# One core, x·W − sub: another order of the transfers, and an eighth pair of tiles transposed on VectorE

## Chip, cores and metric

One NeuronCore of a Trainium2 chip runs the whole kernel. The metric is the device time of one execution in microseconds; the figure shown is the median of several runs.

## What is computed

```
batch, m, k, n = 16, 512, 1024, 768
x (batch, m, k), weight (k, n), sub_value (batch, m, n), all float32
out = (np.matmul(x, weight) - sub_value).astype(np.float32)
```

x, read as 8192 rows of 1024, is 33.6 MB; weight is 3.1 MB; sub_value and out are 25.2 MB each. Together 87.03 MB cross between HBM and SBUF.

## The kernel before

**Tiles.** The 8192 rows are 64 tiles of 128 rows, numbered 0 to 63. Eight tiles (a group of 1024 rows) are interleaved, so that partition p holds eight neighbouring rows of a group, and a transfer of n tiles of one group moves n·4 KB (x) or n·3 KB (sub_value, out) per partition in one packet.

**Work of a tile.** A tile of x lands as float32 in `x_ring` (16 slots). ScalarE casts it to f16 (`cast`, L295). Then it has to be transposed, in one of two ways. On TensorE: four matmuls against an identity (`transposes`, L313; two f16 move as one float32 word) into PSUM `pt_b`, and ScalarE copies the result to `xt_b` (L320, "evac"). Or on VectorE: the tiles whose pair begins in `ON_DVE` are transposed two at a time by sixteen 32-row stream transposes (`transposes_dve`, L340) from `x16p_b` to `xtp_b`. Then TensorE does 16 matmuls of 128x384 (`matmuls`, L364 weight loads and L176 matmuls) with the f16 weight in `w_sb`, into one of three PSUM buffers `po_b` (NPO = 3). VectorE subtracts (`finish`, L384) in place in `so_ring` (32 slots of 128x768), where sub_value had landed, and the slot is then written out.

**Order on TensorE.** The first three tiles follow the weight chunks by hand, with idle matmuls (L401, L414) that fill waits. From tile 3 on, the four transposes of tile mi + 2 stand between the four quarters of the matmuls of tile mi. A tile of a VectorE pair has no transposes on TensorE. Casts are queued 4 tiles ahead of their use, those of a VectorE pair 7 tiles ahead (`lead`). The sixteen stream transposes of a pair are put on VectorE's queue four at a time (PER = 4), each four behind a `finish`, starting at tile (pair − 6).

**Order of the transfers.** One list, `TRANSFERS`, names every DMA in order: kind (x, w, s for sub_value, o for out), first tile, number of tiles. SyncE issues them all, in this order, on one queue (L240 for w, L276 for the others). An x transfer waits until the casts of the tiles that had its slots are done; an s transfer waits until the o transfer that had its slots has landed; an o transfer waits for the `finish` of its tiles. Whatever stands behind a waiting transfer in the list waits too. The first four weight chunks are staged in the last slots of `so_ring`.

**End.** Transfers share semaphores (`lane`). SyncE waits at the end for all output transfers but the last, then the program's closing steps run, and the last transfer is waited for behind them.

Of the kernel before, what the change touches and what calls it, by code (L numbers as in the profile page):

```python
# [19 lines left out]
LEAD_DVE = 7  # L20
PER = 4
HEAD = 3
ON_DVE = frozenset(range(18, 60, 6))
LOOP = None

TRANSFERS = [
    ('x', 0, 1), ('w', 0, 1), ('x', 1, 1), ('w', 1, 1), ('x', 2, 1), ('w', 2, 1),
    ('w', 3, 1), ('x', 3, 2), ('s', 0, 1), ('x', 5, 3), ('s', 1, 3), ('x', 8, 3),
    ('s', 4, 4), ('x', 11, 5), ('s', 8, 8), ('x', 16, 8), ('x', 24, 3), ('s', 16, 8),
    ('x', 27, 5), ('o', 0, 8), ('s', 24, 8), ('x', 32, 8), ('s', 32, 8), ('o', 8, 8),  # L30
    ('x', 40, 8), ('s', 40, 8), ('x', 48, 8), ('o', 16, 8), ('o', 24, 8), ('s', 48, 8),
    ('x', 56, 8), ('s', 56, 8), ('o', 32, 8), ('o', 40, 8), ('o', 48, 8), ('o', 56, 4),
    ('o', 60, 2), ('o', 62, 1), ('o', 63, 1),
]


# [66 lines left out]
def kernel(  # L103
# [174 lines left out]
    def cast(mi):  # L278
# [4 lines left out]
        waits = [landed["x", mi]]  # L283
        if first in ON_DVE:
            if mi == first:
# [14 lines left out]
    def transposes(mi):  # L300
        def one(c):
            def f():
                waits = []
                if c == 0:
                    b, before = take("pt", NPT, mi)
                    waits.append((counter["cast"], cast_at[mi]))
                    if before is not None:
                        waits.append((counter["evac"], evac_at[before]))
                b = slot["pt", mi]
                words = pt_b[:, b].bitcast(F32)[:, c * P : (c + 1) * P]  # L310
                from_ = x16_b[:, slot["x16", mi]].bitcast(F32)[:, c * P : (c + 1) * P]
                last = c == n_c - 1
                pe.add(lambda: nc.tensor.transpose(words, from_, ident), waits, count("turn") if last else None)  # L313
                if last:
                    turn_at[mi] = so_far["turn"]
                    d, before = take("xt", NXT, mi)
                    waits = [(counter["turn"], turn_at[mi])]
                    if before is not None:
                        waits.append((counter["mul"], mul_at[before]))
                    act.add(lambda: nc.scalar.copy(out=xt_b[:, d], in_=pt_b[:, b]), waits, count("evac"))  # L320
                    evac_at[mi] = so_far["evac"]
            return f
        return [one(c) for c in range(n_c)]

    def transposes_dve(mi):

        x16 = x16p_b[:, slot["x16p", mi]].bitcast(F32).rearrange("p j (c q) -> p (j c) q", c=n_c)
        blocks = [(a, b) for a in range(P // Q) for b in range(P // Q)]

        def one(n, a, b):  # L330
            def f():
                waits = []
                if n == 0:
                    d, before = take("xtp", NXTP, mi)
                    waits.append((counter["cast"], cast_at[mi + 1]))
                    if before is not None:
                        waits.append((counter["mul"], mul_at[before + 1]))
                xt = xtp_b[:, slot["xtp", mi]].bitcast(F32).rearrange("p j (c m) -> p (j c) m", c=n_c)
                last = n == len(blocks) - 1
                dve.add(lambda: nc.vector.transpose(  # L340
                    xt[b * Q : (b + 1) * Q, :, a * Q : (a + 1) * Q],
                    x16[a * Q : (a + 1) * Q, :, b * Q : (b + 1) * Q],
                ), waits, count("pair") if last else None)
                if last:
                    pair_at[mi] = so_far["pair"]
            return f
        return [one(n, a, b) for n, (a, b) in enumerate(blocks)]

    def matmuls(mi, c):
        first = mi - mi % 2  # L350
        on_dve = first in ON_DVE
        waits = []
# [26 lines left out]
    def finish(mi):  # L379
        assert mi in done["s"]  # L380
        done["finish"].add(mi)
        o = so_ring[:, mi % NSO].rearrange("p (h n) -> p h n", h=2)
        po = po_b[:, slot["po", mi]]
        dve.add(lambda: nc.vector.tensor_tensor(  # L384
            out=o, in0=po[:, :, :NS], in1=o, op=mybir.AluOpType.subtract
        ), [landed["s", mi], (counter["mul"], mul_at[mi])], count("finish"))
        finish_at[mi] = so_far["finish"]
        issue()
# [16 lines left out]
    def lead(mi):  # L405
        return LEAD_DVE if mi - mi % 2 in ON_DVE else TA + CA

# [38 lines left out]
    for mi in range(HEAD, n_mt):  # L446
# [3 lines left out]
        t = mi + TA  # L450
        tr = transposes(t) if t < n_mt and t - t % 2 not in ON_DVE else []
        for c in range(n_c):
# [6 lines left out]
        finish(mi)  # L459
        if mi + LEAD_DVE - 1 in ON_DVE:  # L460
            waiting += transposes_dve(mi + LEAD_DVE - 1)
# [55 lines left out]
```

## Time and profile before

| what | us |
|---|---|
| median of 3 runs (210.75, 210.76, 211.0) | 210.76 |
| the profiled execution's own time | 211.0 |
| span of that execution in the trace | 208.9 |
| TensorE busy (share of the span) | 197.5 (95%) |
| VectorE busy | 114.0 (55%) |
| ScalarE busy | 113.0 (54%) |
| the data queue (q1), share of the 16 DMA engines' span | 97.9% |
| mean rate of all transfers | 417 GB/s |

The span runs from the first to the last instruction in the trace; 2.1 us of the execution's time lie outside it. Busy times of TensorE are longer than the pace at which matmuls follow each other, because matmuls overlap: a 128x384 matmul shows 326 ns, and 36 of them end to end take 5.85 us in the chain of work, which is 0.163 us each. "Landing" of a transfer is the time at which the last of its 16 parts (one for each DMA engine) has told of its end.

### The profile page before, as it was taken

The page shows a single profiled execution, that of the slowest core. Times are in us where ns is not written, and L with a number is a line of the kernel's source. Part 1 is how long each engine was busy: PE and PEld are TensorE (multiplying, and loading weights), DVE is VectorE, ACT ScalarE, POOL GpSimd, SP SyncE. Part 2 cuts the span into 40 slices and gives each one's busy share as a digit, 9 for nine tenths or more (in the row PEclk, how much of TensorE's full clock was granted, in tenths as well). Part 3 has the DMA queues.
Part 4 walks back from the last instruction along what each step waited for, and adds up shares of the span by engine and source line. Part 5 has one row for each costly group of instructions (what it writes and reads, how often), then busy time and mean ns, then how long its engine had stood idle before and what let it go on. Part 6 is the DMA issues. An engine that isn't in the chain of part 4 may idle for free.

```text
span 208.9 us, 2462 instructions
## 1 busy us (share of the span) xinstructions
PE 197.5 (95%) x1250; PEld 80.1 (38%) x738; DVE 114.0 (55%) x186; ACT 113.0 (54%) x115; POOL 0.7 (0%) x6
## 2 busy tenths in 40 slices
PE   7898799999979999999999999999999999999991
PEld 2432244444333344344344334434434433444430
DVE  0342225106149849929956965992994796332331
ACT  3645665575396274655727628465572751755510
POOL 1000000000000000000000000000000000000000
PEclk9999999999999999999999999999999999999999
DMA  6999999999999999999999999999999999999994
GB/s 209 422 425 425 423 436 431 438 439 436 394 449 421 440 417 425 445 445 406 422 438 438 434 425 442 439 409 438 423 427 445 439 422 431 419 425 442 423 386 192
DMA packets 5626, 87.17 MB, mean 417 GB/s; under 512 B 624, under 2 KB 624, under 8 KB 2032
## 3 DMA queue, kind: packets, MB, share of 16 engines
q1 hardware_dynamic: 5616, 87.03, 97.9%
q8 instruction: 7, 0.11, 0.2%
q14 instruction: 3, 0.02, 0.0%
HBM read 61.87 MB, written 25.17 MB: 417 GB/s over the span
## 4 chain that ended last, share of the span: by engine, by line
PE 68%; DMA 18%; DVE 5%; SPq 3%; ACT 1%; issue 1%; DVEq 0%; ACTq 0%
PE po_b L176 61%; DMA so_ring<-in_sub_value_dram 18%; PE pt_b L313 7%; DVE xtp_b L340 3%; SPq L276 2%; DVE so_ring L384 2%; SPq L240 1%; ACT xt_b L320 0%; ACT x16p_b L295 0%; ACT x_b L295 0%; SPq L512 0%; DVEq L56 0%; ACTq L56 0%; SPq L130 0%
## 5 line engine op out<-in xcount | busy, mean ns | idle before, releaser
L176 PE MATMUL po_b<-w_sb,xt_b 128*128 128x384 f16 x800 | 145.7, 326 | 1.9 <-ACT xt_b L320 1.4
L384 DVE TENSOR_TENSOR so_ring<-po_b,so_ring 128x768 f32<-128x768 f32 x64 | 60.7, 956 | 60.7 <-PE po_b L176 40.1
L320 ACT COPY xt_b<-pt_b 128x1024 f16<-128x1024 f16 x50 | 50.6, 1012 | 72.7 <-PE pt_b L313 72.1
L364 PEld LDWEIGHTS <-xt_b 128*128 128x128 f16 x400 | 39.2, 98 | 58.9 <-issue 53.6
L340 DVE STREAM_TRANSPOSE xtp_b<-x16p_b 32x256 f32<-32x256 f32 x112 | 48.8, 436 | 19.1 <-ACT x16p_b L295 17.3
L313 PE MATMUL pt_b<-ident,x_b 128*128 128x128 f32 x200 | 52.4, 274 | 3.1 <-ACT x_b L295 2.9
L295 ACT CAST x_b<-x_ring 128x1024 f16<-128x1024 f32 x50 | 51.6, 1048 | 6.5 <-DMA x_ring<-in_x_dram 6.5
L313 PEld LDWEIGHTS pt_b<-ident,x_b 128*128 128x128 f32 x200 | 27.5, 141 | 46.8 <-issue 40.4
L176 PE MATMUL po_b<-w_sb,xtp_b 128*128 128x384 f16 x224 | 42.9, 326 | 0.3 <-DVE xtp_b L340 0.3
L295 ACT CAST x16p_b<-x_ring 128x1024 f16<-128x1024 f32 x14 | 14.6, 1046 | 7.0 <-DMA x_ring<-in_x_dram 7.0
L364 PEld LDWEIGHTS <-xtp_b 128*128 128x128 f16 x112 | 11.0, 98 | 13.2 <-issue 11.2
L243 DVE CAST w_sb<-so_ring 128x768 f16<-128x768 f32 x8 | 4.1, 556 | 10.4 <-DMA so_ring<-in_weight_dram 10.4
L401 PE MATMUL po_b<-idle_x,idle_w 128*128 128x512 f16 x25 | 7.5, 449 | 1.5 <-DVE idle_x L395 1.5
L401 PEld LDWEIGHTS po_b<-idle_x,idle_w 128*128 128x128 f16 x25 | 2.7, 112 | 4.6 <-issue 1.9
L295 ACT ACT_TABLE_LOAD x1 | 1.3, 1283 | 0.9 <-SPq L130 0.9
L394 DVE MEMSET idle_w<- 128x64 uint32 x1 | 0.1, 112 | 1.0 <-SPq L130 1.0
L414 PE MATMUL po_b<-idle_x,idle_w 128*128 128x512 f16 x1 | 0.4, 379 | 0.0
L165 POOL TENSOR_SCALAR_AFFINE_SELECT ident<-ident 128x128 f32<-128x128 f32 x1 | 0.3, 294 | 0.1
L395 DVE MEMSET idle_x<- 128x256 uint32 x1 | 0.3, 272 | 0.0
L164 POOL MEMSET ident<- 128x128 f32 x1 | 0.2, 206 | 0.5 <-SPq L130 0.5
L414 PEld LDWEIGHTS po_b<-idle_x,idle_w 128*128 128x128 f16 x1 | 0.1, 98 | 0.1
L501 POOL MEMSET const-bfloat16-1.0<- 128x1 bf16 x1 | 0.1, 102 | 0.0
(3 smaller groups left out, 0.3 us busy)
## 6 DMA issues: line engine op xcount, KB each, us to landing
so_ring<-in_sub_value_dram SPq DMA_DIRECT2D x7, 3072.0 KB, 24.5
out_dram<-so_ring SPq DMA_DIRECT2D x7, 3072.0 KB, 31.2
x_ring<-in_x_dram SPq DMA_DIRECT2D x5, 4096.0 KB, 22.8
x_ring<-in_x_dram SPq DMA_DIRECT2D x2, 2560.0 KB, 26.2
x_ring<-in_x_dram SPq DMA_DIRECT2D x3, 1536.0 KB, 22.4
so_ring<-in_weight_dram SPq DMA_DIRECT2D x4, 768.0 KB, 8.5
x_ring<-in_x_dram SPq DMA_DIRECT2D x3, 512.0 KB, 6.1
so_ring<-in_sub_value_dram SPq DMA_DIRECT2D x1, 1536.0 KB, 26.3
```

Source lines behind the costliest of these rows:

```text
L176: return nc.tensor.add_instruction(mybir.InstMatmult(name=nc.get_next_instruction_name(), engine=full.engine, ins=list(full.ins), outs=lis ...
L240: sp.add(lambda st=st, at=at: nc.sync.dma_start(out=st, in_=w_c[at]), then=(sem, 16))
L243: lambda at=at, r=r, st=st: nc.vector.tensor_copy(out=w_sb[:, at, r], in_=st[:, r]),
L276: sp.add(lambda here=here, there=there: nc.sync.dma_start(out=here, in_=there), waits, (sem, 16))
L295: act.add(lambda: nc.scalar.copy(out=to, in_=x_in), waits, count("cast"))
L313: pe.add(lambda: nc.tensor.transpose(words, from_, ident), waits, count("turn") if last else None)
L320: act.add(lambda: nc.scalar.copy(out=xt_b[:, d], in_=pt_b[:, b]), waits, count("evac"))
L340: dve.add(lambda: nc.vector.transpose(xt[b * Q : (b + 1) * Q, :, a * Q : (a + 1) * Q], x16[a * Q : (a + 1) * Q, :, b * Q : (b + 1) * Q],), ...
L364: pe.add(lambda weights=weights: nc.tensor.ldweights(weights, tile_position=(0, 0)), [w for w in waits if w[0] in ready])
L384: dve.add(lambda: nc.vector.tensor_tensor(out=o, in0=po[:, :, :NS], in1=o, op=mybir.AluOpType.subtract), [landed["s", mi], (counter["mul"] ...
L401: lambda: nc.tensor.matmul(po_b[:, NPO - 1, 0], idle_w, idle_x, start=True, stop=True),
L414: pe.add(lambda: nc.tensor.matmul(po_b[:, NPO - 1, 0], idle_w, idle_x, start=True, stop=True), [(counter["ident"], 2)])
```

## The change

Two constants differ. `ON_DVE` holds one pair more, tiles 12 and 13, so that eight pairs in place of seven are transposed on VectorE. `TRANSFERS` keeps its first eight entries; behind them the same tiles are cut and ordered otherwise. There are 39 transfers in both lists. The function bodies are the same.

```diff
-ON_DVE = frozenset(range(18, 60, 6))
+ON_DVE = frozenset(range(12, 60, 6))
 TRANSFERS = [
     ('x', 0, 1), ('w', 0, 1), ('x', 1, 1), ('w', 1, 1), ('x', 2, 1), ('w', 2, 1),
-    ('w', 3, 1), ('x', 3, 2), ('s', 0, 1), ('x', 5, 3), ('s', 1, 3), ('x', 8, 3),
-    ('s', 4, 4), ('x', 11, 5), ('s', 8, 8), ('x', 16, 8), ('x', 24, 3), ('s', 16, 8),
-    ('x', 27, 5), ('o', 0, 8), ('s', 24, 8), ('x', 32, 8), ('s', 32, 8), ('o', 8, 8),
-    ('x', 40, 8), ('s', 40, 8), ('x', 48, 8), ('o', 16, 8), ('o', 24, 8), ('s', 48, 8),
-    ('x', 56, 8), ('s', 56, 8), ('o', 32, 8), ('o', 40, 8), ('o', 48, 8), ('o', 56, 4),
-    ('o', 60, 2), ('o', 62, 1), ('o', 63, 1),
+    ('w', 3, 1), ('x', 3, 2), ('s', 0, 2), ('x', 5, 3), ('s', 2, 3), ('x', 8, 5),
+    ('s', 5, 3), ('x', 13, 3), ('s', 8, 4), ('x', 16, 8), ('s', 12, 4), ('s', 16, 4),
+    ('x', 24, 8), ('s', 20, 4), ('s', 24, 8), ('o', 0, 8), ('x', 32, 8), ('s', 32, 8),
+    ('x', 40, 8), ('o', 8, 8), ('x', 48, 8), ('s', 40, 8), ('o', 16, 8), ('o', 24, 8),
+    ('s', 48, 8), ('x', 56, 8), ('o', 32, 8), ('s', 56, 8), ('o', 40, 8), ('o', 48, 8),
+    ('o', 56, 5), ('o', 61, 2), ('o', 63, 1),
 ]
```

## Prediction

> **What bounds the kernel now.** I read the page first: TensorE's busy share and the row of the DMA engines.
>
> ```profile
> PE 197.5 (95%) x1250; PEld 80.1 (38%) x738; DVE 114.0 (55%) x186; ACT 113.0 (54%) x115; POOL 0.7 (0%) x6
> ...
> DMA  6999999999999999999999999999999999999994
> ...
> q1 hardware_dynamic: 5616, 87.03, 97.9%
> ```
>
> Two resources are full at once. The data queue has no empty slice between the first and the last, and TensorE looks full too. So the end decides, and I read there the chain of work, the issues of the last transfers (start on SyncE; size and time from issue to landing), and the engines by stretch.
>
> ```profile
> 199.10 5.21 PE po_b L176 x32
> 204.31 0.02 issue
> 204.34 0.96 DVE so_ring L384
> ```
>
> ```profile
> 202.72 0.33 SPq L276 DMA_DIRECT2D out_dram<-so_ring  x1
> ```
>
> ```profile
> 205.32 0.33 SPq L276 DMA_DIRECT2D out_dram<-so_ring  x1
> ```
>
> ```profile
> out_dram<-so_ring SPq DMA_DIRECT2D x1, 768.0 KB, 5.6
> ```
>
> ```profile
> out_dram<-so_ring SPq DMA_DIRECT2D x1, 384.0 KB, 3.8
> ```
>
> ```profile
> out_dram<-so_ring SPq DMA_DIRECT2D x1, 384.0 KB, 2.3
> ```
>
> ```profile
> 203.00:204.00 1.00, 1.00 (x8) 0.29 (x3) 0.00 (x0) 0.00 (x0) 0.00 (x0) 1.00 0.85 347
> 204.00:205.00 1.00, 0.30 (x2) 0.00 (x0) 0.67 (x1) 0.00 (x0) 0.00 (x0) 1.00 0.78 316
> 205.00:206.00 1.00, 0.00 (x0) 0.00 (x0) 0.29 (x1) 0.00 (x0) 0.00 (x0) 1.00 0.39 157
> 206.00:207.00 1.00, 0.00 (x0) 0.00 (x0) 0.00 (x0) 0.00 (x0) 0.00 (x0) 1.00 0.86 341
> ```
>
> TensorE ends at 204.3, the subtraction of tile 63 at 205.30, its output is issued at 205.32 and lands 2.3 us later, at 207.63 by the trace's landing events. The outputs before it were issued long before their landing: tiles 60 and 61 landed at 205.59, tile 62, issued at 202.72, at 206.51. Tile 62 took 0.92 us behind its predecessor: the bytes of one tile, with no pause. Had tile 63 been ready, it would have landed at 206.51 + 0.92 = 207.43. The last transfer thus waited only 0.20 us for TensorE. The DMA shares of 0.39 to 0.85 do not speak against that: the landing events of one transfer are spread over 2.32 us between the first and the last DMA engine (tiles 60 and 61: 203.27 to 205.59), so the early engines idle in the tail while the last one has work.
>
> Why is one engine that late? The spread is 0.86 us until 24.85 us and 2.11 for the transfer that lands at 29.80. In between lies this stretch (27.5 to 28.8 us):
>
> ```profile
> q1 hardware_dynamic: 55, 0.55, 102.8%
> q8 instruction: 1, 0.02, 5.1%
> ```
>
> A 16 KB instruction packet, 1.06 us in the trace, ran on one engine, and that engine's share of x tiles 8 to 10 landed 1.2 us late; the engine kept that lag. There are seven such packets, about 25 us apart. By the end seven of 16 parts come 1.55 us or more behind the first, so each packet seems to have met another engine.
>
> **The change, part by part.** *Pair 12 on VectorE.* It removes eight transposes from TensorE. In the chain one is a step of 0.11 us ("PE pt_b L313"), so 0.88 us less. ScalarE loses two evacuations of 1.01 us, and has room (54%). VectorE gets 16 stream transposes of 0.436, 7.0 us. Their cover: x 13 lands at 39.6 (below), is cast by 40.7; four groups of 1.8 us with `finish` of tiles 7 to 9 (0.96 each) between them end near 51. TensorE reaches tile 12 near 51.6. Queued behind the waiting transposes are those `finish`; tile 10's matmuls need that of tile 7, done near 43.5 and wanted at 46.4. So nothing is added, but the cover is 0.6 us, and whatever exceeds it is a wait of TensorE.
>
> *The order.* Landing times follow by adding packet times behind the unchanged x 3,4 (17.39): 8 packets per engine of 122 ns (3 KB), 234 (6), 351 (9), 462 (12), 766 (20), 912 (24), 1213 (32). That gives s 0 at 19.3, x 5 at 22.95, s 2 at 25.7, x 8 to 12 at 31.9, with the instruction packet's 1.2 at 33.05, s 5 at 35.9, x 13 at 39.6, s 8 at 43.2, x 16 at 52.9, s 12 at 56.6, s 16 at 60.3, x 24 at 70.0, s 24 at 81.0, x 32 at 98.0, x 40 at 115.0, o 8 at 122.3, x 48 at 132.0, s 40 at 139.3, x 56 at 170.9, s 56 at 185.5, o 48 at 200.1. Against TensorE:
>
> ```profile
> 23.91 0.33 PE L313 MATMUL pt_b<-ident,x_b 128*128 128x128 f32 x1 [1.40 <-ACT x_b L295]
> ```
>
> ```profile
> 58.48 0.82 PE L176 MATMUL po_b<-w_sb,xt_b 128*128 128x384 f16 x4 [1.37 <-ACT xt_b L320]
> 70.55 0.82 PE L176 MATMUL po_b<-w_sb,xtp_b 128*128 128x384 f16 x4 [0.29 <-DVE xtp_b L340]
> ```
>
> The wait at 23.91 stays: the cast began at 22.81, when ScalarE was free, and x 5 now lands at 22.95. The waits at 58.48 and 70.55 go (x 16 lands at 52.9 where it was 56.44); by the starts of matmuls, counting the small gaps around them and the one at 47.5, that is 2.5 us. A new wait comes: x 8 lands at 33.05 where it was 29.80, its cast ends at 34.15, and TensorE wants the transpose at 33.08: 1.1 us. From tile 12 on x and s stay ahead of TensorE; s 40 and s 56 land about 3.4 us after their tiles' matmuls, which VectorE feels, but the third `po_b` buffer still has over a us to spare. So TensorE ends at 204.3 − 0.88 − 2.5 + 1.1 = 202.0, and without the DMA engines the last output would land at 202.0 + 0.04 + 0.96 + 0.02 + 2.31 = 205.3.
>
> *The queue's own end.* All bytes still pass. Cutting them otherwise changes the sum of packet times by 24 ns (8 × (6.158 − 6.155 us) over the sizes that differ). The queue must not run dry: the tightest issue is x 48, behind cast 39, done at 120.5 before and 2.4 earlier now, 118.2; it moves 1.4 us after issue (2.31 − 0.92), 119.6, and o 8 keeps the last engine until 122.3. The waits of s 40, s 48 and s 56 for landed outputs have a transfer of 7 us or more queued ahead. The last outputs (5, 2, 1 tiles) are issued near 194.9, 200.6 and 203.2, each over 2 us before its turn. So the last landing is 207.43 + 0.02, a gain of 0.2 us, of TensorE's 2.3 us. The closing steps follow the landing before the last by 0.8 us (206.53 to 207.31), as now.
>
> Bounds of that gain: below, nothing (another cut that costs 0.2), above 2.3 (queue no limit). I take 0.2, since the landing events give the queue's pace directly.
>
> One rule speaks against it. The Trainium skill, "DMA: Bandwidth & Descriptors", Where 436 GB/s comes from, states a ceiling of 435.2 GB/s; the 24 KB packets here run at 431 (16 × 24576 B / 912 ns). At 435.2 the 200 us of traffic would take 1.8 us less, and the gain would be near 2. The rows are used.
>
> A second: "Runtime: NRT & Kernel Launch", Instruction fetch mechanics, calls the crossing of a 16 KiB block mostly hidden. The landing 1.2 us late says otherwise where the queue is full; by the page the end would come 1.2 us sooner.
>
> **The rivals.** *Floor holds* (forecast): 210.76 − 0.2 = 210.6; the profiled execution would show 208.7 and 210.8. A TensorE that gains nothing from the new order (x 8's wait eats it) ends here too, up to 0.2 later.
>
> *The queue gives way*, 0.36: the last engine's lag is not the same (an instruction packet misses it, 1.2 us), or the unprofiled queue is a little quicker (0.3% is 0.6 us). Then TensorE's lead counts, up to 210.76 − 2.3 = 208.4; most of it I place at 209.7 to 210.3. For it: the spread was 0.86 without such packets. Against it: no slice of the DMA row but the first and the last has room.
>
> *Slower*, 0.14: with other timing two instruction packets meet one engine. Its lag becomes 2.3 + 1.1, the end 208.5, the time 211.7. It decides from 0.6 us of extra lag on. Against it: seven packets on seven engines here. A dry queue at x 48, which needs TensorE 2.7 us late, is the lesser part.
>
> **The numbers.** A measurement of this kernel tells 0.2%, 0.42 us, from no change: 210.34 to 211.18. The floor's case (0.50) lies inside it. Faster is 0.36, slower 0.14. The range 209.7 to 211.2 holds the floor's case, some 0.28 of the second and little of the third. The floor's own range is 210.4 to 211.0.
>
> **What would show it.** Right: TensorE's last matmul near 202, no wait at 58 or 70, a wait of 1 us near 34, last output issued near 203.2 but landing near 207.4, spread of the landings 2.3. Wrong: a last landing before 206.8 or after 208; an empty slice in the DMA row; TensorE ending after 203.5.

## Result and profile after

The changed kernel takes 211.5 us (median of 4 runs, 211.47 to 212.05) against 210.83 for the kernel before (4 runs): a ratio of 1.0037, 95% interval 1.0019 to 1.0055. It is slower by 0.37%, and outside the range of the prediction (209.7 to 211.2). The profiled execution took 211.47 us, its span is 209.7 where it was 208.9.

The page of the changed kernel, busy time of TensorE, the DMA row, the rate in GB/s in the same 40 slices, and the data queue:

```profile
PE 197.3 (94%) x1242; PEld 79.3 (38%) x730; DVE 120.6 (57%) x202; ACT 110.8 (53%) x113; POOL 0.7 (0%) x6
...
DMA  5999999999999999999999999999999999999994
GB/s 204 419 427 430 440 406 431 445 427 414 417 455 418 435 439 424 452 425 416 456 419 406 456 425 414 427 375 431 431 434 444 427 419 436 430 436 422 432 408 177
...
q1 hardware_dynamic: 5616, 87.03, 97.9%
```

The queue is as full as before. But one inner slice moves 375 GB/s, the 27th, 136 to 141 us; in the kernel before no inner slice but the last full one was below 394. The DMA row shows nothing there: an engine whose packet takes longer counts as busy.

The end of the chain of work, and issue and time to landing of the last two outputs:

```profile
197.90 5.21 PE po_b L176 x32
203.12 0.02 issue
203.14 0.96 DVE so_ring L384
```

```profile
201.52 0.33 SPq L276 DMA_DIRECT2D out_dram<-so_ring  x1
```

```profile
out_dram<-so_ring SPq DMA_DIRECT2D x1, 768.0 KB, 5.9
```

```profile
204.12 0.33 SPq L276 DMA_DIRECT2D out_dram<-so_ring  x1
```

```profile
out_dram<-so_ring SPq DMA_DIRECT2D x1, 384.0 KB, 4.3
```

TensorE ends 1.2 us earlier than before (203.1 for 204.3), but the last output now stands in the queue: issued at 204.12, it lands 4.3 us later, at 208.39 by the landing events, 0.94 behind the transfer ahead of it (207.45). Before it landed at 207.63. So the queue sets the end, as forecast, but the last output lands 0.94 us later than worked out (forecast 207.45; that the transfer ahead of it landed at the same 207.45 is chance).

Where it lost that stands between two landings: x 48 lands at 132.13 (forecast 132.0), s 40 at 140.44 (forecast 139.3). Those are 8.31 us for a transfer that takes about 7.28 everywhere else, 1.03 too long. All later transfers are 1.0 us late and keep their pace: o 16 7.28, o 24 7.27, s 48 7.28, x 56 9.69. The rest of the list before it was within 0.4 us of the forecast (furthest off is x 13, 39.2 for 39.6; x 8 at 32.75, x 16 at 52.99, s 24 at 80.92, x 40 at 115.14, o 8 at 122.44). In this trace one stretch of the queue accounts for the difference.

The waits of TensorE after (timeline, then the table of waits):

```profile
24.07 0.33 PE L313 MATMUL pt_b<-ident,x_b 128*128 128x128 f32 x1 [1.56 <-ACT x_b L295]
33.87 0.33 PE L313 MATMUL pt_b<-ident,x_b 128*128 128x128 f32 x1 [0.46 <-ACT x_b L295]
```

```profile
PE po_b L176 <- DVE so_ring L384: 1.0, 1, 1.0
```

The waits at 58 and 70 are gone, and the new one near 34 is there. The last line is one that was not forecast: TensorE waits at 140 for the subtraction of tile 40, which waits for s 40. It is a consequence of the lost microsecond, not its cause, since the queue has lost it before.

What slows in it? The trace's packets show it: on each of the 16 DMA engines one 24 KB packet of s 40, begun between 136.0 and 137.2 us, takes 1.1 to 2.0 us, where 0.91 is usual. When o 16 begins to move, near 138, all packets take 0.91 again.

### The profile page after: what moved, and what is told of

Read it like the earlier page. It is cut to its first block, busy times and chain, and to the rows that moved or that the text cites. A ratio compares the mean times of both kernels' runs of the same rounds, so it can differ in the third digit from the quotient of the medians.

```text
span 209.7 us, 2461 instructions
## 1 busy us (share of the span) xinstructions
PE 197.3 (94%) x1242; PEld 79.3 (38%) x730; DVE 120.6 (57%) x202; ACT 110.8 (53%) x113; POOL 0.7 (0%) x6
## 4 chain that ended last, share of the span: by engine, by line
PE 51%; DMA 35%; DVE 6%; SPq 2%; ACT 2%; issue 1%; DVEq 0%; ACTq 0%
PE po_b L176 46%; DMA out_dram<-so_ring 14%; DMA x_ring<-in_x_dram 12%; DMA so_ring<-in_sub_value_dram 9%; PE pt_b L313 6%; DVE xtp_b L340 3%; DVE so_ring L384 3%; SPq L276 2%; ACT x_b L295 1%; SPq L240 1%; ACT xt_b L320 0%; ACT x16p_b L295 0%; SPq L512 0%; DVEq L56 0%; ACTq L56 0%
## 5 line engine op out<-in xcount | busy, mean ns | idle before, releaser
L176 PE MATMUL po_b<-w_sb,xt_b 128*128 128x384 f16 x768 | 138.8, 326 | 0.0
L320 ACT COPY xt_b<-pt_b 128x1024 f16<-128x1024 f16 x48 | 48.6, 1012 | 67.8 <-PE pt_b L313 67.0
L340 DVE STREAM_TRANSPOSE xtp_b<-x16p_b 32x256 f32<-32x256 f32 x128 | 55.8, 436 | 13.9 <-ACT x16p_b L295 11.8
L364 PEld LDWEIGHTS <-xt_b 128*128 128x128 f16 x384 | 37.7, 98 | 56.9 <-issue 53.3
L295 ACT CAST x_b<-x_ring 128x1024 f16<-128x1024 f32 x48 | 49.4, 1048 | 10.2 <-DMA x_ring<-in_x_dram 10.1
L313 PE MATMUL pt_b<-ident,x_b 128*128 128x128 f32 x192 | 50.2, 274 | 3.2 <-ACT x_b L295 3.0
L176 PE MATMUL po_b<-w_sb,xtp_b 128*128 128x384 f16 x256 | 49.1, 326 | 1.1 <-DVE so_ring L384 1.0
L313 PEld LDWEIGHTS pt_b<-ident,x_b 128*128 128x128 f32 x192 | 26.4, 141 | 45.0 <-issue 38.4
L295 ACT CAST x16p_b<-x_ring 128x1024 f16<-128x1024 f32 x16 | 16.7, 1046 | 9.3 <-DMA x_ring<-in_x_dram 9.3
L364 PEld LDWEIGHTS <-xtp_b 128*128 128x128 f16 x128 | 12.5, 98 | 16.0 <-issue 13.6
```

The costliest lines, as they stand in the source:

```text
L176: return nc.tensor.add_instruction(mybir.InstMatmult(name=nc.get_next_instruction_name(), engine=full.engine, ins=list(full.ins), outs=lis ...
L295: act.add(lambda: nc.scalar.copy(out=to, in_=x_in), waits, count("cast"))
L340: dve.add(lambda: nc.vector.transpose(xt[b * Q : (b + 1) * Q, :, a * Q : (a + 1) * Q], x16[a * Q : (a + 1) * Q, :, b * Q : (b + 1) * Q],), ...
L364: pe.add(lambda weights=weights: nc.tensor.ldweights(weights, tile_position=(0, 0)), [w for w in waits if w[0] in ready])
```

## Experiments

Throughout, "s 40" is the time from the mean landing of the transfer ahead of it (over its 16 parts) to its own; 7.3 to 7.4 us is the pace. In the changed kernel it is 7.88, a loss of 0.6 in the mean of the engines; the engine that lands last lost 1.03. "Lead" is the time from the issue of a transfer to the first landing of the one ahead of it, which is when the first of the DMA engines has nothing else left.

**The order, the pair, one place of the order.** Theory A was that s 40 is slow because of where it stands in the list; B that the memory slows by chance; C that the eighth pair's timing does it. Four kernels on one chip, against 211.12 us for the kernel before there. The changed kernel again:

> The changed kernel once more. Theory A (the queue slows while s 40 is read between x 48 and o 16, because of this place in the list): again about 0.9 us too long between the landings of x 48 and s 40 (8.3 us where 7.3 is the pace), last landing near 208.4, 211.5 us. Theory B (the memory slows by chance, at times of its own): the slow stretch stands elsewhere or is missing; where it is missing the last landing is near 207.45 and the time 210.6.

Measured: 212.26 us, ratio 1.0043 (1.0017 to 1.0068). s 40 takes 8.15 us, between 136 and 139 again; last landing 209.08. The stretch comes again in the same place, so B falls.

```diff
-ON_DVE = frozenset(range(12, 60, 6))
+ON_DVE = frozenset(range(18, 60, 6))
```

> The new order with the old seven pairs. Theory A: the slow stretch at s 40 stays, 211.5 us; TensorE ends 0.9 us later than in the changed kernel, near 204, without effect. Theory C (the slow stretch comes of the eighth pair's timing on the engines): no slow stretch, last landing 207.45, 210.6 us. Theory B: no rule.

Measured: 213.1 us, ratio 1.0093 (1.0064 to 1.0122). s 40 takes 8.57 us, and x 48 ahead of it 10.45 where 9.7 is the pace. C falls; but the expectation for the end missed, since more is lost here than in the changed kernel, and TensorE, at 206.9, is late too. The new order without the eighth pair is worse than with it.

In the old order, the eighth pair alone (`ON_DVE` from 12):

> The old order with eight pairs. Theory A: no slow stretch of 0.9 us (s 40 is followed by x 48); TensorE waits for pair 12, whose x lands at 39.4 as before and whose s 8 to 15 block VectorE until 46.7, so about 0.4 us later at the end: 211.1 us. Theory C: a slow stretch near 136 us, 211.5 us or more. Theory B: no rule.

Measured: 211.65 us, ratio 1.0031 (1.0005 to 1.0056). s 40 takes 7.31 us. TensorE waits 2.4 us at 38.8, ends at 204.5, and the last output lands at 208.18. No slow stretch, as A and not C expected; but the time is 0.5 us above the 211.1 expected. TensorE ends only 0.2 us later than in the kernel before, and the last DMA engine is 2.8 us behind the first from x 48 on, where it was 2.3. The pair gains nothing in the old order.

```diff
-    ('x', 40, 8), ('o', 8, 8), ('x', 48, 8), ('s', 40, 8), ('o', 16, 8), ('o', 24, 8),
+    ('o', 8, 8), ('x', 40, 8), ('s', 40, 8), ('x', 48, 8), ('o', 16, 8), ('o', 24, 8),
```

> The changed kernel with the old order in one place only: o 8, x 40, s 40, x 48 in place of x 40, o 8, x 48, s 40. Theory A: the slow stretch at s 40 goes, last landing near 207.45, 210.6 us. Theory B and C: nothing changes, 211.5 us, the slow stretch near 136 us or elsewhere.

Measured: 210.99 us, ratio 1.0007 (0.9986 to 1.0028). s 40 takes 7.40 us and no stretch is slow. The profiled execution's last landing, 208.15, is not at 207.45: there the last DMA engine is 2.8 us behind the first from 170 us on, against 2.3. So this one place of the order carries the loss, and A stands as far as that. What about the place does it?

**Addresses.** Theory D: reading that group of sub_value collides with something else in memory. E: it is the place in the list. In all three kernels only the line that forms `there` changes, for groups 5 and 7 of all arrays, groups 2 and 6 of out, and groups 5 and 7 of sub_value:

```diff
-            there = view[at // S][:, at % S : at % S + n]
+            there = view[{5: 7, 7: 5}.get(at // S, at // S)][:, at % S : at % S + n]
```

> The changed kernel, with row groups 5 and 7 of x, sub_value and out exchanged: tiles 40 to 47 stand for group 7, 56 to 63 for group 5; the order in time, the sizes and the waits stay. Theory D (addresses: reading group 5 of sub_value while group 2 of out is next collides in memory): the slow stretch at s 40 goes, last landing near 207.45, 210.6 us; it might come at s 56. Theory E (the place in the list, whatever the addresses): s 40 still takes 8.0 us or more from first landing to first landing, 211.5 us.

> The changed kernel, with the writes of out's groups 2 and 6 exchanged (tiles 16 to 23 are written to group 6 and 48 to 55 to group 2, so that out is not in the reference's order); nothing else changes. Theory D: the slow stretch at s 40 goes, 210.6 us. Theory E: s 40 still takes 8.0 us or more, 211.5 us.

> The changed kernel, with the reads of sub_value's groups 5 and 7 exchanged (so that out is off by the difference of the two); x and out stay. Theory D: the slow stretch at s 40 goes, 210.6 us. Theory E: s 40 still takes 8.0 us or more, 211.5 us.

Measured, a single run of each, beside 210.93 us for the kernel before: s 40 takes 8.13, 8.30 and 8.13 us (7.92, 8.14 and 7.89 from first landing to first landing), the times are 211.55, 212.12 and 212.93 us, and the slow stretch is at 135 to 139 in each. D falls.

```diff
-    ('x', 40, 8), ('o', 8, 8), ('x', 48, 8), ('s', 40, 8), ('o', 16, 8), ('o', 24, 8),
+    ('x', 40, 8), ('o', 8, 8), ('x', 48, 8), ('s', 40, 4), ('o', 16, 8), ('s', 44, 4), ('o', 24, 8),
```

> The changed kernel with s 40 cut in two: x 48, s 40 (4 tiles), o 16, s 44 (4 tiles), o 24. Theory E, if the turn from a read of s to o 16 is what slows: some slow stretch stays, before o 16, 211.0 to 211.5 us. Theory D: a slow stretch may stay. If what slows is that s 40 is a long read with all of o 16 and o 24 queued behind: none, 210.6 us. TensorE's wait of 1.2 us at 140 goes in any case, since s 40 lands near 136.

Measured: 212.07 us, ratio 1.0056 (1.0039 to 1.0073). s 40, now half, takes 4.59 us where 3.7 is the pace, and the slow stretch moved with it, to 132 to 135. So it belongs to the queue and not to a point of time or of the engines' work, and a transfer of half the length pays no less (0.9 us; r1, whole, 0.86). TensorE's wait at 140 is gone and the time is no better: that wait was not what cost it.

**The late issue.** What is special about the place can be the time of issue. SyncE issues x 48 behind cast 39, which TensorE's progress sets. In the changed kernel and in the one before:

```profile
117.99 0.33 SPq L276 DMA_DIRECT2D x_ring<-in_x_dram  x1
```

```profile
120.58 0.33 SPq L276 DMA_DIRECT2D x_ring<-in_x_dram  x1
```

It is issued earlier now than it was. But before, s 40 was still in the queue ahead of it, until 127.5 on the first engine: a lead of 6.9 us. Now o 8 is all that is left, until 120.38: a lead of 2.4. In e1 the lead was 0.9, and the loss the largest. Theory F: the late issue upsets the queue. G: s 40 directly ahead of o 16 is slow. H: it is slow because it is issued at the moment o 8 lands.

```diff
-    ('x', 48, 8), ('s', 40, 8),
+    ('x', 48, 4), ('x', 52, 4), ('s', 40, 8),
```

> The changed kernel with x 48 in two transfers of 4 tiles, in its place; the first needs only cast 35 and is issued some 10 us earlier, so that the queue is never close to dry before s 40. Theory F (the late issue of x 48, about 2.3 us before the first DMA engine has nothing left, upsets the queue, and s 40 pays): no slow stretch at s 40, last landing near 207.5, 210.6 us. Theory G (s 40 directly ahead of o 16 is what slows): s 40 still 0.6 to 1.0 us too long, 211.5 us.

Measured: 210.79 us against 211.06, ratio 0.9984 (0.997 to 0.9998). s 40 takes 7.30 us; the last output lands at 207.68. The engines by stretch, the last number the rate, first of the changed kernel:

```profile
127.00:130.00 3.00, 3.00 (x22) 1.34 (x12) 2.90 (x7) 1.92 (x3) 0.00 (x0) 1.00 0.88 377
133.00:136.00 3.00, 3.00 (x20) 0.95 (x10) 2.90 (x7) 3.00 (x4) 0.00 (x0) 1.00 0.94 401
136.00:139.00 3.00, 3.00 (x21) 1.07 (x10) 0.39 (x1) 0.26 (x1) 0.00 (x0) 1.00 1.09 377
```

and of the one with the halves:

```profile
133.00:136.00 3.00, 3.00 (x20) 0.88 (x9) 2.92 (x6) 3.00 (x4) 0.00 (x0) 1.00 1.05 451
136.00:139.00 3.00, 3.00 (x21) 1.13 (x11) 0.54 (x2) 0.42 (x1) 0.00 (x0) 1.00 1.07 459
```

From 133 to 139 the other engines' work is the same to 0.2 us, and the rate differs. The rate of 3 us alone proves little, though: the first line, 127 to 130, shows 377 too, and there x 48 keeps its pace (9.65 us). It is the packets that tell: the halved kernel has none of the slow ones. The halved kernel is 0.16% faster than the kernel before. But the spans of both, medians of these 10 and 13 executions, are 209.0 us, and its last landing, 207.68, is not ahead of the 207.63 before; the difference lies in what is outside the span (1.8 and 2.0 us). So the loss is gone, and the gain of the forecast (a last landing at 207.45, a span of 208.7) is not shown.

```diff
-    ('x', 40, 8), ('o', 8, 8), ('x', 48, 8), ('s', 40, 8), ('o', 16, 8), ('o', 24, 8),
+    ('o', 8, 8), ('x', 40, 8), ('x', 48, 8), ('s', 40, 8), ('o', 16, 8), ('o', 24, 8),
```

> The changed kernel with o 8 ahead of x 40; x 48 is issued as late as before, s 40 right behind it (o 8 has landed long ago) and still directly ahead of o 16. Theory F: s 40 still 0.6 to 1.0 us too long. Theory G: likewise. Theory H (s 40 is issued at the moment when o 8 has landed, and that is what slows it): no slow stretch, last landing near 207.5.

Measured: 210.87 us in a single run; s 40 takes 7.87 us with x 48 issued 2.3 us ahead. H falls: here s 40 is issued 0.4 us behind x 48, 12 us before its turn, when o 8 has long landed. The last output lands at 207.77, because the last DMA engine happens to be only 1.9 us behind the first.

```diff
-    ('x', 40, 8), ('o', 8, 8), ('x', 48, 8), ('s', 40, 8), ('o', 16, 8), ('o', 24, 8),
+    ('o', 8, 8), ('x', 40, 8), ('s', 40, 8), ('o', 16, 8), ('x', 48, 8), ('o', 24, 8),
```

> The changed kernel with o 8, x 40, s 40, o 16, x 48, o 24: s 40 directly ahead of o 16, both issued 17 us before their turn. Its end is late, since x 48 comes late for TensorE (worked out: last landing near 211). Read it at s 40 alone. Theory G: s 40 0.6 to 1.0 us too long. Theories F and H: s 40 takes 7.3 us.

Measured: s 40 takes 7.40 us (the time, 215.56 us, is that of TensorE's wait for x 48, 5.2 us at 143.5; TensorE's wait was expected smaller, last landing 211 for 212.5). G falls.

**Lead by itself.** Halving x 48 had changed two things, the lead and the size of the packets ahead of s 40 (theory I). So the halves were kept and the second one held back, by a wait on the 37th subtraction (h1, below) or on the 36th (h2); and in a third kernel x 48 stayed whole, with o 16 put ahead of it.

```diff
+            if kind == "x" and at == 52:
+                waits.append((counter["finish"], 37))
```

> As the halved x 48, but the second half waits for one more event, the subtraction of tile 36 (the 37th), which ends near 124.3: issued some 0.9 us before the first DMA engine has nothing left. Theory F (a late issue upsets the queue): s 40 is again 0.6 us or more too long, or x 52 itself. Theory I (it was the one transfer of 32 KB per partition ahead of s 40 that slowed it): s 40 takes 7.3 us as in the halved kernel, and x 52 loses at most the 0.5 us in which the queue stands empty (issue to movement is 1.4).

> The same with the subtraction of tile 35 (the 36th), near 121.3: issued 3.9 us before the first engine has nothing left. Theory F: s 40 too long by something between 0 and 0.6 us. Theory I: 7.3 us.

```diff
-    ('x', 40, 8), ('o', 8, 8), ('x', 48, 8), ('s', 40, 8), ('o', 16, 8), ('o', 24, 8),
+    ('x', 40, 8), ('o', 8, 8), ('o', 16, 8), ('x', 48, 8), ('s', 40, 8), ('o', 24, 8),
```

> The changed kernel with x 40, o 8, o 16, x 48, s 40, o 24: x 48 whole and issued at 118 as before, but with o 16 still to go in the queue, 9.6 us. Its end is late, since s 40 lands 7.3 us later than TensorE wants it (worked out: last landing 212.4). Read it at s 40 alone. Theory F: s 40 takes 7.3 us. Theory I: 0.6 us or more too long.

Measured, all kernels together, in the order of the lead:

| kernel | transfer ahead of s 40 | its lead, us | its own time, us (pace) | s 40, us |
|---|---|---|---|---|
| h1 | x 52, 4 tiles | 0.8 | 5.98 (4.98) | 8.30 |
| e1 | x 48, 8 tiles | 0.9 | 10.45 (9.7) | 8.57 |
| r1 | x 48 | 1.9 | 9.94 | 8.15 |
| f4, f1, f5 | x 48 | 2.2 to 2.3 | 9.6 to 9.7 | 8.30, 8.13, 8.13 |
| g2 | x 48 | 2.3 | 9.80 | 7.87 |
| changed kernel | x 48 | 2.4 | 9.65 | 7.88 |
| k1 (below) | x 48 | 2.6 | 9.65 | 7.64 |
| h2 | x 52, 4 tiles | 3.8 | 4.98 | 7.30 |
| g1 | x 52, 4 tiles | 7.0 | 4.99 | 7.30 |
| h3 | x 48 | 9.6 | 9.58 | 7.33 |

h1 and h2 differ only in the event that one wait on SyncE names (so that s 40 and o 16, behind x 52 in the list, are issued 2.1 and 2.2 us later in h1 as well), and s 40 takes 8.30 in the one and 7.30 in the other. The rate of h1 in the two stretches shown above:

```profile
133.00:136.00 3.00, 3.00 (x20) 0.88 (x9) 2.91 (x6) 3.00 (x4) 0.00 (x0) 1.00 1.07 451
136.00:139.00 3.00, 3.00 (x22) 1.16 (x11) 0.48 (x2) 0.37 (x1) 0.00 (x0) 1.00 0.93 270
```

h3 has x 48 whole, issued at 118.10 as in the changed kernel, and s 40 behind it at its pace. Theory I falls and F stands. That h2 should lose something between 0 and 0.6 us was answered with 0: the limit lies between leads of 2.6 (k1, below) and 3.8 us. Below it the loss doesn't follow the lead closely (8.30 and 7.87 at 2.2 and 2.3), and most rows are single runs. The times are 213.56 us (h1), 211.33 (h2) and 218.09 (h3, TensorE waits 7.3 us for s 40; its last landing, 215.0, is later than the 212.4 worked out), beside 211.17 for the kernel before. Two things bound theory F. In h2 another read, s 56, which stands directly ahead of o 40, takes 0.4 us too long, with packets of up to 1.7 us near 182, and no late issue is near it; the theory has no answer to that. And a write issued as late costs nothing here: the last outputs of the changed kernel, o 61 and o 63, are issued 1.55 and 0.79 us before the first engine runs out, o 48 of h3 1.49, and none loses more than 0.1 us. What is shown is a loss behind a late read.

**Two more on the mechanism.** First the outputs behind s 40 were held until 131.8:

```diff
-                waits.append((counter["finish"], max(finish_at[t] for t in need)))
+                waits.append((counter["finish"], 39 if at == 16 else max(finish_at[t] for t in need)))
```

> The changed kernel with o 16 (and o 24 behind it) held until the subtraction of tile 38 (the 39th) near 131.8, so that only x 48 and s 40 are in the queue from 122 to 132; o 16 is still issued 6 us before its turn. Theory J (the outputs queued behind s 40 slow it): s 40 takes 7.3 us. Theory K (the late issue of x 48 alone does it): s 40 again 0.6 us or more too long.

Measured: s 40 takes 7.64 us, 0.36 above the 7.28 of its packets, and the lead was 2.6; 211.26 us, beside 210.94 for the kernel before. It answers neither J nor K clearly: less was lost, and the lead was a little longer too.

Then the old order, with x 48 held back:

```diff
+            if kind == "x" and at == 48:
+                waits.append((counter["finish"], 37))
```

> The kernel before with x 48 (behind s 40 there) held until the subtraction of tile 36 (the 37th) near 126.7, 0.8 us before the first DMA engine has nothing left. Theory F, in its general form: x 48 loses about 0.5 us and one of the transfers behind it is slow by 0.6 us or more, though the order is the old one; last landing 208.5 or later. If only s 40 between x 48 and o 16 can be slowed: nothing but the 0.5 us, which the last output's wait for TensorE hides in part, last landing near 208.0.

Measured: 214.33 us; lead 0.9; x 48 takes 11.78 us where 9.7 is the pace, and the transfers behind it keep theirs. It has two slow stretches, one as it begins, and one at its end, which again stops as o 16 begins to move:

```profile
127.00:130.00 3.00, 3.00 (x22) 1.31 (x13) 1.15 (x3) 2.87 (x4) 0.00 (x0) 1.00 1.02 385
130.00:133.00 3.00, 3.00 (x22) 1.31 (x13) 2.90 (x7) 1.89 (x2) 0.00 (x0) 1.00 0.94 393
133.00:136.00 3.00, 3.00 (x21) 1.26 (x12) 2.91 (x6) 1.00 (x2) 0.00 (x0) 1.00 1.22 448
136.00:139.00 3.00, 3.00 (x21) 0.88 (x9) 2.89 (x6) 1.90 (x3) 0.00 (x0) 1.00 0.82 240
139.00:142.00 3.00, 3.00 (x21) 1.11 (x11) 1.92 (x2) 0.00 (x0) 0.00 (x0) 1.00 0.85 363
```

So the old order is harmed by a late read as the new one is; from x 5 on it never had one (5.0 us is the shortest lead of a read). The loss was larger than expected, and it fell on x 48, which here stands directly ahead of the next write, and not on a transfer behind it. In all kernels that issue x 48 or x 52 with a lead of 2.6 us or less it is the last 3 us of reads ahead of the next write that slow; where the lead is under 1 us, the first packets of the late read too. Why the queue pays so late, 9 us and more after the issue, stays open: no run shows what the engines lack there.

## Why the prediction was wrong

**What held.** The two bounds, and that the queue's own end would set the time: TensorE lost its waits at 58 and 70, ended earlier, and the last output waited in the queue. The landing times worked out from packet sizes were within 0.4 us up to x 48. The spread of the landings at the end is 2.5 us (2.3 forecast), and the closing steps again follow the landing before the last by 0.8 us.

**The step that failed.** It is "the queue must not run dry: the tightest issue is x 48 ... o 8 keeps the last engine until 122.3". The issue came when it was worked out (117.99 for 118.2), and the spare time was counted to the last DMA engine, 2.7 us, and taken as free of cost. Two things were wrong in it. The first engine has nothing left 2 us earlier than the last, at 120.38, so the spare was only 1 us by the same sum. That alone did no harm: no engine has a gap between its packets from 112 to 126 us, so the queue did not run dry. But a read issued just in time is not free: with x 48 or x 52 issued 0.8 to 2.6 us before the first engine's end, 0.36 to 1.3 us were lost at s 40 in every kernel of the table (2.1 at x 48 in k2), and with 3.8 us or more none there. The term was put at 0 and measures 1.03 between the last landings; 207.45 + 1.03 is 208.48, and the last landing is 208.39.

**The rivals.** The slower end was named with a place (x 48) and given as the lesser part of 0.14, with a point from which it decides, TensorE 2.7 us late, that was wrong; TensorE was not late at all. Its main part, two instruction packets on one engine, did not happen in the changed kernel: there are seven such packets again, and 2.5 us of spread. The prediction's reading of these packets was off: it counted seven late parts at the end and gave each packet one engine, but of the 16 landings it read (tiles 60 and 61) nine come 1.55 us or more behind the first, and seven are early. So the seven packets don't explain every late engine. Nor did the second rival (a queue that gives way) come: in g1, where the late issue is removed, TensorE ends at 201.9 and the last output still lands at 207.68. So the floor held there; its 0.2 us do not show in the span.

**TensorE's sum.** It ends at 203.1 where 202.0 was forecast: 1.16 us is the wait at 140 for s 40, 0.2 one at 173, and 0.2 more at 24; the wait for x 8 was 0.5 smaller (0.63 for 1.1, by the starts of the matmuls). The third `po_b` buffer was said to have over a us to spare at s 40; that was wrong. In g1, where s 40 keeps its pace, the subtraction of tile 40 ends at 140.21 and TensorE starts with that buffer at 140.56: 0.35 us to spare. So in the changed kernel nearly all of the microsecond lost in the queue became a wait of TensorE. None of that reached the end.

**The two rules of the Trainium skill.** The ceiling of "DMA: Bandwidth & Descriptors", Where 436 GB/s comes from, decided nothing: 24 KB packets again take 0.912 us, 431 GB/s, 1% under it, and the landing times are those of the rows. The other page calls the cost of crossing a 16 KiB boundary mostly hidden ("Runtime: NRT & Kernel Launch", Instruction fetch mechanics); it says so of the stream of instructions, not of the data queue. In the data queue it is again not hidden: x 8 lands at 32.75, 0.9 us behind the 31.9 of its packet times, with the instruction packet at 27.70.

## What to carry to other kernels

Where one queue carries the whole kernel, a change of order is to be costed by the lead of every read, taken to the moment when the first DMA engine runs out and not the last, and some 4 us of it are to be kept; here 2.4 us cost 1 us and 3.8 cost nothing. Writes at the end of the list needed no such lead. A transfer that waits on the compute engines can be halved, so that both halves are issued with more lead. A gain on an engine that shares the bound is worth only what the other bound leaves: the 2.4 us that TensorE ends earlier in g1 brought 0.3 us of the time and nothing of the span.

## What the runs showed of the hardware that was not expected

A read issued 0.8 to 2.6 us before the first DMA engine had nothing left made a read slow later on: 24 KB packets of 0.91 us took 1.1 to 2.4, on all 16 engines in the changed kernel (on 13 and 15 in k1 and g2, which lost least), for some 3 us, 9 us and more after the issue, and only until the next write began to move. In the changed kernel no engine stands idle where the late read begins, nor where the packets are slow; only their length and the landings give it away. The rate of those 3 us, 240 to 377 GB/s in the changed kernel, r1, g2, h1 and k2, can be read as low only beside them, since 377 was also seen at full pace.
